# A list scheduler that counts a TensorE instruction as ready a margin behind its inputs, and a sample's loads traced one stretch later

## The chip, the cores and the metric

The kernel runs on one NeuronCore of a Trainium2 chip. The metric is device time in microseconds of one launch. A profiled execution gives a trace; its times count from the first instruction of the span. The engines are called PE (TensorE, matrix products; PEld is its weight load, which is an instruction of its own), DVE (VectorE), ACT (ScalarE), POOL (GpSimd) and SP (SyncE, which here issues every DMA). Each engine works through its own list of instructions in the order of that list.

## The reference, cut to what matters

One layer of a streaming encoder is run for a prompt of 1024 frames and for a sample of 64 new frames with caches, with the same weights:

```python
h = rms_norm(xp, g_norm1)
qa, ka, va, qb, kb, vb, logf = in_proj(h, w_in, ...)       # 8 heads A, 8 heads B, forget logits
oa = chunk_band_attn_prompt(qa, ka, va, rel_bias)          # band of 64-frame chunks, 8 chunks back
ob = forget_attn_prompt(qb, kb, vb, logf)                  # causal, cumulative forget bias
xp = xp + concat(oa, ob) @ w_o
mk, mv = mem_kv(mem_prompt, g_mem, w_mkv, g_mk)            # memory keys and values, 256 tokens
xp = xp + mem_attend(rms_norm(xp, g_norm2), mk, mv, w_mq, g_mq, w_mo)
f, conv = conv_ffn(rms_norm(xp, g_norm3), zeros, w_up, w_conv, b_conv, w_down)
xp = xp + f
# the same for the sample xs (64 frames), whose attention reads cache_a_k/v (512 rows),
# cache_b_k/v (1024 rows) and cache_mem_k/v, and whose conv reads state_conv
```

Outputs are both streams, the new keys, values and forget logits, the memory keys and values and the conv states. All is float32. The kernel makes most products as three products of split operands (`SPLIT`: high x high, low x high, high x low), which is why an operand appears as a pair such as `whi` and `wlo`.

## The kernel before

**Stages.** The program is traced, that is, written down instruction by instruction, in this order. (1) A ramp: the first projections (`pj`) and their splits. (2) For each pair of heads in turn, projections of eight 128-frame tiles, and beside them the attention of the pairs before: scores into the one tile `S` (`Attn.score`, L706), the minimum over them (`mx`, L709), the exponential (L711), transposes (`PT`, L743), their split into `pth` and `ptl` (L744, L745), and the products with `v` into `O` (L762). The queries `q` come from transposes into `tq` (L484) and two evictions (L493, L495). (3) The memory products: eight column blocks `n` of `w_mkv`, two row tiles each, in pieces of six matmuls (`mem_piece`, L829); weights come by `load_wm` (tile `mwraw`, L813) and are split on ACT and DVE (L821, L822). Beside them stand the eight samples, that is, the sample's eight pairs of heads. (4) The output product (`w_o`), memory attention and the first half of `w_mo`. (5) From `arranged` on, products of a Strassen-like scheme for the feed-forward part, in the order in which they are written.

**The samples.** `Sample.load` issues on SP the loads of one pair: `sqd` and `svn` (its own queries, keys and values, by way of DRAM), two halves of the cached keys `kraw`, and one (A) or two (B) tiles `vraw` of cached values. `load_bias` loads its bias `s` (from `rows` for A, from `negs` for B). `prep` transposes `sqd` (L1022), scales it (L1027, L1028) and, for B, works the bias over on POOL (L1031, L1034). `score` makes the products with `kraw` (L1045, L1046), the minima on DVE (L1048, L1050) and the exponential on ACT (L1056). `turn` transposes (L1069) and copies (L1073 and L1071), `sum` multiplies with `vraw` and `svn` (L1083), `out` transposes back (L1093). The order of the pairs is `SAMPLES`, B pairs first: samples 0 to 3 are B, 4 to 7 are A. Samples 0 to 3 have three `kraw` buffers, 4 to 7 four of their own.

A loop over `x` makes one stretch for each sample: it traces the score of sample `x`, the turns and sums of the sample before and the prep of sample `x + 1`, woven (`weave`) with `PER[x]` pieces of the memory products from `line`. At its head stand the bias load of sample `x + 1` and, before the change, the loads of sample `x + 3`. Samples 0, 1 and 2 are loaded earlier. In stretches 5 and 6 `load_early` loads the first tiles of the output product (`oraw`, `omix`).

**The planner.** What is traced is not what runs. At the end `arrange(tc, arranged)` takes everything traced before `arranged` (stages 1 to 4) and gives each of the five engines a new order, by simulating a list schedule. Each instruction is a node with an assumed busy time and an assumed time to its result (`cost`). Node numbers follow the traced order and are the priority: of the instructions that are ready on an engine, the one traced first goes first. A node is ready when all that it depends on is done in the simulation (results on other engines plus `signal`, 0.07 us) and when its tile has a free buffer; for a matmul behind a matmul it depends on, when that one is streamed. An SP instruction has one more condition: the matmul traced `AHEAD` (10) products ahead of it must have begun. The loop takes the engine that can start earliest. Instructions whose time has not come are in `coming[engine]`; those that are ready are in the two heaps of `waiting[engine]`, called `a` and `b` (`b` for those that need a port shared by DVE and POOL). The result is written as an order of each engine and nothing more: on the chip the engines wait by semaphores for what they need, in that order, whether or not the planned times come true.

Of the kernel before, what the change touches and what calls it, by code (L numbers as in the profile page):

```python
# [41 lines left out]
def hybrid_step(ctx: ExitStack, tc: tile.TileContext, i: dict, o: dict):  # L42
# [345 lines left out]
    def weave(main, subs):  # L388
        j = 0
        for x, f in enumerate(main):  # L390
            f()
            while j * len(main) < len(subs) * (x + 1):
                subs[j]()
                j += 1
        for f in subs[j:]:
            f()
# [539 lines left out]
    kvs, stores, waiting = {}, [], []  # L936
# [193 lines left out]
    samples = [Sample(p) for p in SAMPLES]  # L1130
# [80 lines left out]
    def open_left():  # L1211
        nonlocal stream
        left.close()
        stream = Stream(late_left.enter_context(tc.tile_pool(name="wr", bufs=1, side="left")))
        x = late_left.enter_context(tc.tile_pool(name="x0", bufs=1, side="left")).tile([P, 384], F32, name="x0")
        ha = mixes.enter_context(tc.tile_pool(name="ha", bufs=1, side="left"))
        stage = rest.enter_context(tc.tile_pool(name="stage", bufs=1, side="left"))
        mixr.extend(parts(ha, "a"))
        raws = dict(enumerate(early_mix))

        def place_of(n):
            c0, cn = CHUNKS[n // KT]
            return n % KT, slice(c0, min(c0 + cn, T))

        def load_mix(n):
            if n < KT:
                return
            k, c = place_of(n)
            raws[n] = stage.tile([P, 384], F32, name="mraw", bufs=STAGE)[:, :c.stop - c.start]
            nc.sync.dma_start(raws[n], mixd[k][:, c])  # L1230

        def split_mix(n):
            k, c = place_of(n)
            hi, lo = (mixr[z][k][:, c] for z in range(2))
            act.copy(hi, raws[n])
            dve.tensor_tensor(lo, raws[n], f32(hi), op=ALU.subtract)  # L1236
            if KT <= n and n + STAGE < 3 * KT:
                load_mix(n + STAGE)

        with tc.issue_after(samples[-1].loaded.ins):  # L1240
            for n in range(KT, KT + STAGE // 2):
                load_mix(n)
            stream.fetch()
            for n in range(KT + STAGE // 2, KT + STAGE):
                load_mix(n)
        nc.sync.dma_start(x, i["xT"][0, :, 0:384])
        assert not waiting
        for f in stores:
            f()
        return ha, [[lambda n=c * KT + k: split_mix(n) for k in range(KT)] for c in range(3)], x  # L1250
# [3 lines left out]
    def load_early(n):  # L1254
        if n < 2:
            raw = mq.tile([P, 4, P], F32, name="oraw", bufs=3)
            nc.sync.dma_start(raw, srcs[n])
            early_raws.append(raw)
        for k in range(4 * n, 4 * n + 4):
            raw = mq.tile([P, 384], F32, name="omix", bufs=KT)  # L1260
            nc.sync.dma_start(raw, mixd[k][:, 0:384])
            early_mix.append(raw)

    old, ha = [], None
    for x in range(len(samples) + 1):
        if not line and ha is None:
            ha, split, early_x = open_left()
            left_at = x
        cur = samples[x] if x < len(samples) else None
        nxt = samples[x + 1] if x + 1 < len(samples) else None  # L1270
        if nxt:
            nxt.load_bias()
        if x + 3 < len(samples):
            samples[x + 3].load()
        if x in (5, 6):
            load_early(x - 5)
        new, fin = [], []
        if cur:
            new = [cur.score]
        if nxt:  # L1280
            fin = [nxt.prep]
        subs = new[:1] + old[:2] + new[1:] + old[2:-1] + fin[:1] + old[-1:] + fin[1:]
        main = line[:PER[x]]
        del line[:PER[x]]
        if ha and x == left_at:
            pieces = first[0].pieces
            subs = new[:1] + old[:2] + split[0][:1] + new[1:] + split[0][1:2]
            subs += [lambda: stream.upto(1)] + old[2:-1] + split[0][2:4] + [lambda: stream.upto(2)]
            subs += [pieces[0], split[0][4], pieces[1], split[0][5]] + old[-1:] + [pieces[2], split[0][6], pieces[3], split[0][7]]
        elif ha:  # L1290
            main = pieces[4:] + [f for two in zip(split[1], first[1].pieces) for f in two]
            subs = [lambda: stream.upto(4)] + subs
        weave(main, subs)
        if cur:
            c = cur.nc
            old = [lambda z=z, u=cur: u.turn(z) for z in range(2)] + [lambda u=cur: u.sum(0)]
            old += ([lambda u=cur: u.turn(2), lambda u=cur: u.sum(1)] if c == 2 else [])
            old += [lambda u=cur, c=c: u.sum(c), cur.out]
# [243 lines left out]
    for n, u in enumerate(mems):  # L1542
        h, c = u.h, u.c
        a, b = (mems[n - 1] if n else None), (mems[n - 2] if n > 1 else None)
# [39 lines left out]
    def long_row(tag):  # L1584
        return row(tag, 768)[:, :H]
# [27 lines left out]
    for w, m in enumerate(ROWS):  # L1613
        x = long_row("qhi")
# [152 lines left out]
    for n, m in enumerate(ROWS):  # L1767
        x = long_row("qhi")
# [270 lines left out]
    for s, (what, f) in enumerate(steps):  # L2039
# [16 lines left out]
        for m in range(4):  # L2056
            two = [(x, z) for x in ((s,) if f < NG - 2 else (s, s + 1)) for z in range(2)]
            for x, z in sorted(two, key=lambda v: v[1]) if m == 3 and what == "M4" else two:
                la, ra = down_ops[x]
                first, final = steps[x][1] == 0, steps[x][1] == NG - 1  # L2060
                if True:
                    for y, (p, b) in enumerate(SPLIT):
                        pe.matmul(ws[m][:, z, :Q], la[p][:, m * P:(m + 1) * P], ra[b][:, z * Q:z * Q + Q],  # L2063
                                  start=first and y == 0 and what in opening, stop=final and y == 2 and what in closing, skip_group_check=True)
# [13 lines left out]
    assert not any(later.values())  # L2078
    late_left.close()
    arrange(tc, arranged)  # L2080


# [4 lines left out]
def arrange(tc, end):  # L2087

    import heapq

    signal = 0.07
    nodes, owner, made, touched, opened, closed = [], {}, {}, {}, {}, []
    writer, readers, group = {}, {}, {}
    setter = select = None
# [49 lines left out]
    for ins in traced[:end]:  # L2144
        engine, kind = str(ins.engine).split(".")[-1], type(ins).__name__
# [77 lines left out]
    after, missing, ready = [[] for _ in nodes], [len(x[2]) + len(x[3]) for x in nodes], [0.0] * len(nodes)  # L2223
    coming, free, order = ({e: make() for e in ENGINES} for make in (list, float, list))
    waiting = {e: ([], []) for e in ENGINES}
# [9 lines left out]
    def release(n):  # L2235
        for t in held[n][1] - taken:
            tag = owner[t][2]
            if not slots[tag]:
                stuck.setdefault(tag, []).append(n)
                return  # L2240
            ready[n] = max(ready[n], min(slots[tag]))
        heapq.heappush(coming[nodes[n][1]], (ready[n], n))
# [9 lines left out]
    def earliest(e):  # L2252
        a, b = waiting[e]
        return min([1e9] + [free[e]] * bool(a) + [max(free[e], port)] * bool(b) + [max(free[e], x[0]) for x in coming[e][:1]])

    while True:
        start, engine = min((earliest(e), e) for e in ENGINES)
        if start == 1e9:
            break
        while coming[engine] and coming[engine][0][0] <= start:  # L2260
            n = heapq.heappop(coming[engine])[1]
            heapq.heappush(waiting[engine][nodes[n][6]], n)
        a, b = waiting[engine]
        line = min([x for x in (a, b if port <= start else []) if x], default=None)
        if line is None:
            continue
        n = heapq.heappop(line)
        order[engine].append(n)
        _, _, _, _, busy, done, shared = nodes[n]
        free[engine] = start + busy  # L2270
        if engine == "SP":
            lane = max(lane, start + 1.4) + done
            done = lane - start + 0.3 + min(0.5, done / 2)
        if shared:
            port = start + busy
        for t in held[n][1]:
            if t not in taken:
                taken.add(t)
                slots[owner[t][2]].remove(min(slots[owner[t][2]]))
            left[t] -= 1  # L2280
            over[t] = max(over[t], start + done + signal)
            if not left[t]:
                slots[owner[t][2]].append(over[t])
                for m in stuck.pop(owner[t][2], ()):
                    release(m)
        for m, begun in after[n]:
            same = nodes[m][1] == engine
            ready[m] = max(ready[m], start + (0 if begun else busy if same and engine == "PE" else done if same and engine != "SP" else done + signal))
            missing[m] -= 1
            if not missing[m]:  # L2290
                release(m)
# [91 lines left out]
```

## Time and profile before

| | |
|---|---|
| time, median of 3 runs | 1693.71 us (1690.34 to 1694.01) |
| time of the profiled execution | 1686.39 us |
| its span, first to last instruction | 1684.6 us |
| mean granted clock of TensorE | 0.999 |
| busy PE / PEld / DVE / ACT / POOL | 1660.5 / 1613.2 / 1166.4 / 907.9 / 583.2 us |
| moved by DMA | 199.82 MB, mean 119 GB/s |

How to read it: the profiled execution is one run; its time holds its span and some 2 us around it. The median of the other runs lies 7.3 us above it. Differences inside the profile are taken within the profile. Rows of the table of windows give, for a stretch of the span, its length and the busy time of PE, PEld, DVE, ACT and POOL with their counts of instructions, then the granted clock, the mean busy share of the DMA engines and GB/s. A row of waits reads: engine, tile and line of the instruction that waited, what it waited for, us in total, times, longest. A row of a timeline gives start, length, engine, line, operation, and in brackets the idle time before it and what ended that.

### The profile page before, as it was taken

To read this page: it belongs to the slowest core of one execution; us is meant where nothing else is said; L and a number is where in the kernel's file an instruction comes from. 1 tells how busy PE (TensorE), PEld (TensorE's weight loads), DVE (VectorE), ACT (ScalarE), POOL (GpSimd) and SP (SyncE) were. 2 spreads that over 40 slices of the span, in tenths; PEclk is the share of its full clock that TensorE was granted. 3 is DMA by queue.
4 is the path that set the end of the run, shared out by engine and by line. 5 is a ranking of instruction groups with operands and counts; after the bars stand their busy time and mean duration, and the time that the engine had idled before them with its cause. 6 is when DMAs were issued, how large, how long until landed. Compare 5 with 4: busy or idle time off the path is not lost.

```text
span 1684.6 us, 33070 instructions
## 1 busy us (share of the span) xinstructions
PE 1660.5 (99%) x12027; PEld 1613.2 (96%) x12027; DVE 1166.4 (69%) x2584; ACT 907.9 (54%) x2003; POOL 583.2 (35%) x846
## 2 busy tenths in 40 slices
PE   9999999999999999999999999999999999999999
PEld 8899899999998879999999999999999999999999
DVE  7866866766778644344553797777777777559996
ACT  8866677767777564345555554333333333444442
POOL 1756688888853213444446111000000000000000
PEclk9999999999999999999999999999999999999999
DMA  7323243232235974421115632222222222983332
GB/s 242 91 77 84 76 113 91 77 92 84 64 118 165 290 216 152 141 82 58 55 58 162 214 115 84 77 78 77 78 77 77 78 78 84 320 298 120 102 109 88
DMA packets 142260, 199.82 MB, mean 119 GB/s; under 512 B 22200, under 2 KB 85304, under 8 KB 142096
## 3 DMA queue, kind: packets, MB, share of 16 engines
q1 hardware_dynamic: 142096, 197.70, 37.8%
q8 instruction: 95, 1.56, 0.4%
q14 instruction: 69, 0.57, 0.1%
HBM read 148.01 MB, written 43.34 MB: 114 GB/s over the span
## 4 chain that ended last, share of the span: by engine, by line
PE 87%; ACT 4%; DVE 4%; DMA 2%; issue 1%; SPq 0%; POOL 0%; DVEq 0%; ACTq 0%; POOLq 0%
PE W L1739 27%; PE W L2063 14%; PE pj L1183 14%; PE pj L413 11%; PE S L706 4%; PE O L762 3%; PE PT L743 3%; PE pj L829 2%; PE W L1183 1%; PE pj L535 1%; PE S L1475 1%; PE tq L1514 1%; PE O L1514 1%; PE tq L484 1%; DMA k<-k 1%
## 5 line engine op out<-in xcount | busy, mean ns | idle before, releaser
L413 PE MATMUL pj<-whi,xhi 128*128 128x384 f32 (+1 forms) x480 | 172.7, 360 | 0.0
L413 PE MATMUL pj<-whi,xlo 128*128 128x384 f32 (+1 forms) x480 | 164.7, 343 | 0.0
L413 PE MATMUL pj<-wlo,xhi 128*128 128x384 f32 (+1 forms) x480 | 164.1, 342 | 0.0
L1739 PE MATMUL W<-h,hi 128*128 128x272 f32 x704 | 134.3, 288 | 1.4 <-ACT qlo L1875 1.4
L1845 POOL COPY s<-gp 128x2 f32<-128x2 f32 x22 | 15.8, 719 | 336.1 <-DVE gp L1844 336.1
L2063 PE MATMUL W<-f,hi 128*128 128x272 f32 x672 | 127.2, 287 | 0.0
L745 DVE TENSOR_TENSOR ptl<-PT,pth 128x512 fp32r<-128x512 f32 (+2 forms) x192 | 97.9, 521 | 32.4 <-ACT pth L744 30.6
L713 POOL TENSOR_SCALAR s<-s,ssum 128x640 f32<-128x640 f32 (+7 forms) x128 | 92.9, 728 | 68.2 <-DVE ssum L712 52.2
L711 ACT ACTIVATE s<-s,mx 128x640 f32<-128x640 f32 (+7 forms) x128 | 94.5, 738 | 35.9 <-DVE mx L709 35.0
L744 ACT CAST pth<-PT 128x512 fp32r<-128x512 f32 (+2 forms) x192 | 84.6, 451 | 54.1 <-PE PT L743 52.4
L1739 PEld LDWEIGHTS W<-h,hi 128*128 128x128 f32 x704 | 110.3, 188 | 1.7 <-ACT qlo L1875 1.6
L2063 PEld LDWEIGHTS W<-f,hi 128*128 128x128 f32 x672 | 105.2, 188 | 0.1
L1739 PE MATMUL W<-h,lo 128*128 128x272 f32 x352 | 101.3, 288 | 0.0
L706 PE MATMUL S<-k,q 128*128 128x256 f32 (+3 forms) x432 | 90.5, 323 | 7.2 <-DVE mx L709 2.8
L2063 PE MATMUL W<-f,lo 128*128 128x272 f32 x336 | 96.7, 288 | 0.0
L1602 ACT CAST hi<-raw 128x512 fp32r<-128x512 f32 x68 | 42.2, 621 | 98.7 <-PE W L1739 59.2
L413 PEld LDWEIGHTS pj<-whi,xhi 128*128 128x128 f32 x480 | 90.6, 189 | 1.5
L413 PEld LDWEIGHTS pj<-wlo,xhi 128*128 128x128 f32 x480 | 90.8, 189 | 0.7
L413 PEld LDWEIGHTS pj<-whi,xlo 128*128 128x128 f32 x480 | 90.3, 188 | 0.4
L743 PE MATMUL PT<-ident,s 128*128 128x128 f32 x528 | 87.6, 273 | 0.8 <-DVE ptl L745 0.8
L706 PEld LDWEIGHTS S<-k,q 128*128 128x128 f32 x432 | 67.3, 188 | 21.8 <-DVE q L495 8.1
L1183 PE MATMUL pj<-a,hi 128*128 128x384 f32 (+1 forms) x352 | 87.2, 332 | 1.0 <-DVE a L1236 0.9
(611 smaller groups left out, 5684.3 us busy)
## 6 DMA issues: line engine op xcount, KB each, us to landing
raw<-in_w_down_dram SPq DMA_DIRECT2D x45, 256.0 KB, 2.7
wraw<-in_w_dram SPq DMA_DIRECT2D x56, 192.0 KB, 2.7
raw<-in_w_up_dram SPq DMA_DIRECT2D x41, 256.0 KB, 2.7
h<-ad SPq DMA_DIRECT2D x32, 272.0 KB, 5.1
mwraw<-in_w_mkv_dram SPq DMA_DIRECT2D x16, 512.0 KB, 5.6
raw<-in_w_mo_dram SPq DMA_DIRECT2D x32, 256.0 KB, 3.2
kvraw<-in_w_down_dram SPq DMA_DIRECT2D x32, 256.0 KB, 3.4
k<-k SPq DMA_DIRECT2D x60, 128.0 KB, 2.4
```

Source lines behind the costliest of these rows:

```text
L413: pe.matmul(pj[:, :nw], x_part(a, k, t * P, P), wt[k][b][:, :nw], start=n == 0, stop=n == 3 * KT - 1)
L706: pe.matmul(sp[:, a:a + m], q, ring[:, h, z, k0:k0 + m], start=z == 0, stop=z == 1)
L711: act.activation(s[:, :n], s[:, :n], ACT.Exp, bias=mx, scale=-1.0, accum_out=sm)
L713: pool.tensor_scalar(s[:, :n], s[:, :n], sm, 1.0, op0=ALU.mult, op1=ALU.mult)
L743: pe.transpose(pt[:, b - ch[0]], self.s[j][:, (b - w0) * P:(b - w0 + 1) * P], ident)
L744: act.copy(hi[:, f:f + n, j], pt[:, f:f + n])
L745: dve.tensor_tensor(lo[:, f:f + n, j], pt[:, f:f + n], f32(hi[:, f:f + n, j]), op=ALU.subtract)
L762: pe.matmul(op[:r, cols], v[:, :r], self.pts[b][m][:, x, cols], start=first and (b, m) == steps[0], stop=ch[-1] == self.last and (b, m) == ...
L1183: pe.matmul(out()[:, :cn], w[a][:, k % 4], x[b][k][:, c0:c0 + cn], start=k == 0 and (a, b) == SPLIT[0], stop=k == KT - 1 and (a, b) == SPL ...
L1602: act.copy(hi, t)
L1739: pe.matmul(w[:, z, :Q], a(p, j), rights[j][b][:, z * Q:z * Q + Q], start=fresh and begin and j == 0 and x == 0, stop=final and end and j ...
L2063: pe.matmul(ws[m][:, z, :Q], la[p][:, m * P:(m + 1) * P], ra[b][:, z * Q:z * Q + Q], start=first and y == 0 and what in opening, stop=fina ...
```

## The change

Two things change.

1. In the planner, `sure` gives PE a margin of 0.2 us. While PE has a ready instruction in `a` or `b`, an instruction in `coming` moves to the ready ones only if its time lies at least 0.2 us before the present start. If PE has nothing ready, the old rule holds. A matmul that depends on a matmul of PE itself gets its time 0.2 us earlier, so that the margin does not apply to it. The other engines have no margin.
2. In the loop over the samples, `samples[x + 3].load()` is traced behind the `weave` of stretch `x` instead of ahead of it.

```diff
-        if x + 3 < len(samples):
-            samples[x + 3].load()
         if x in (5, 6):
             load_early(x - 5)
...
         weave(main, subs)
+        if x + 3 < len(samples):
+            samples[x + 3].load()
...
-    signal = 0.07
+    signal, sure = 0.07, {"PE": 0.2}
...
-        while coming[engine] and coming[engine][0][0] <= start:
+        a, b = waiting[engine]
+        while coming[engine] and coming[engine][0][0] <= start - (sure.get(engine, 0.0) if a or b else 0.0):
             n = heapq.heappop(coming[engine])[1]
             heapq.heappush(waiting[engine][nodes[n][6]], n)
-        a, b = waiting[engine]
...
-            ready[m] = max(ready[m], start + (0 if begun else busy if same and engine == "PE" else done if same and engine != "SP" else done + signal))
+            ready[m] = max(ready[m], start + (0 if begun else busy - sure[engine] if same and engine == "PE" else done if same and engine != "SP" else done + signal))
```

## The prediction, as put on record before the change was run

> **What bounds the kernel now.** I read the page first: the busy times and the chain that ended last.
>
> ```profile
> span 1684.6 us, 33070 instructions
> PE 1660.5 (99%) x12027; PEld 1613.2 (96%) x12027; DVE 1166.4 (69%) x2584; ACT 907.9 (54%) x2003; POOL 583.2 (35%) x846
> PE 87%; ACT 4%; DVE 4%; DMA 2%; issue 1%; SPq 0%; POOL 0%; DVEq 0%; ACTq 0%; POOLq 0%
> ```
>
> TensorE is the bound. No multiplication is added or taken away, so only time in which PE stands still can be won or lost: 1684.6 - 1660.5 = 24.1 us of visible idle time, and whatever hides inside a "busy" PE, since a matmul's modelled end covers short gaps. Next, the table of windows, cut where the stages of the program change:
>
> ```profile
> 0.00:20.00 20.00, 17.93 (x96) 17.60 (x97) 13.72 (x35) 15.91 (x35) 0.70 (x6) 1.00 0.92 308
> 20.00:60.00 40.00, 35.69 (x219) 32.32 (x217) 35.57 (x121) 37.13 (x106) 21.88 (x31) 1.00 0.51 151
> 60.00:520.00 460.00, 455.53 (x3013) 430.60 (x3014) 331.69 (x920) 325.76 (x837) 347.65 (x544) 1.00 0.31 86
> 520.00:640.00 120.00, 112.34 (x800) 100.11 (x799) 74.54 (x211) 76.37 (x213) 20.83 (x30) 0.99 0.80 236
> 640.00:950.00 310.00, 309.62 (x2093) 304.10 (x2092) 139.02 (x367) 152.99 (x360) 140.53 (x143) 1.00 0.36 111
> 950.00:1684.60 734.60, 729.34 (x5816) 728.47 (x5814) 571.84 (x934) 299.78 (x458) 51.57 (x94) 1.00 0.35 116
> ```
>
> The columns are length, busy time of PE, PEld, DVE, ACT and POOL, the granted clock, the DMA share and GB/s. Visible PE idle is 2.1 us at the start, 4.3 in the ramp, 4.5 in the long stage of projections with attention beside them, 7.7 in the stage of memory products and samples (DMA share 0.80), 0.4 after it, 5.3 in the rest. The planner whose rule is changed orders only what is traced before about 950 us, so 18 to 19 us of visible idle lie in its reach. PEld, the weight loads, shows more: 29.4 us idle in 60:520. The waits of PEld there, and in 640:950:
>
> ```profile
> PEld S L706 <- DVE q L495: 8.1, 23, 0.8
> PEld S L706 <- DVE mx L709: 4.4, 8, 0.7
> PEld PT L1498 <- POOL s L1490: 3.7, 20, 0.4
> ```
>
> So 31 scores (L706) were issued before their input was there, for 8.1 + 4.4 = 12.5 us, 0.40 us each: either q had just been written or the one score tile had just been read out. One such place on the timeline, below the row of one of the three kinds of projection matmuls in that stage:
>
> ```profile
> L413 PE MATMUL pj<-whi,xhi 128*128 128x384 f32 x448 | 161.2, 360 | 0.0
> 364.62 0.34 PE L413 MATMUL pj<-whi,xlo 128*128 128x384 f32 x1
> 364.62 0.19 PEld L413 LDWEIGHTS pj<-whi,xhi 128*128 128x128 f32 x1
> 364.79 0.34 PE L413 MATMUL pj<-whi,xhi 128*128 128x384 f32 x1
> 365.48 0.30 PEld L706 LDWEIGHTS S<-k,q 128*128 128x128 f32 x2 [0.67 <-DVE mx L709]
> 365.48 0.51 PE L706 MATMUL S<-k,q 128*128 128x512 f32 x1 [0.35 <-DVE mx L709]
> ```
>
> Projection matmuls start 0.17 us apart (364.62, 364.79); the score starts 0.69 later. PE lost 0.69 - 0.17 = 0.52 us where PEld shows 0.67 idle: a wait of PEld costs PE its length less 0.15. Other projections were ready, but the engine takes its list in order.
>
> **The change, part by part.**
>
> Part 1, the margin. While PE has something ready, the planner now offers it only what was ready 0.2 us before (the diff's figure, about one weight load of the rows, 0.19). A just-ready score then stands one or two matmuls later. Nothing is added on the chip: no instruction, no wait, no DMA; PE's successors of its own matmuls are exempted (busy - 0.2). What a later score costs is covered by projections, 1344 of which (448 of each kind) stand in this stage; without that cover (ramp, end of attention) the rule does not apply, for it needs another ready instruction.
>
> (a) 60:520: the 31 waits cost PE 31 x (0.40 - 0.15) = 7.8 us. A margin of 0.2 takes at most 0.2 from each and nothing from those under 0.15; I take 0.15 on average, 31 x 0.15 = 4.6 us. Ends: 0, if the delay moves with the plan, and 7.8.
>
> (b) 640:950: 20 transposes (L1498) waited for POOL for 3.7 us, 0.185 each; by the same rule 20 x 0.035 = 0.7 us. Ends 0 and 3.7, the whole wait.
>
> (c) 20:60: ACT and DVE are over 88% busy and PE rarely has a choice. I take 0.5 of the 4.3 us; ends a loss of 1 (a new order of a latency chain) and a gain of 2.
>
> (d) 520:640: the waits of PE are few and long.
>
> ```profile
> PE S L706 <- DMA k<-k: 2.1, 1, 2.1
> PE PT L977 <- DVE kv L958: 1.7, 1, 1.7
> PE O L1083 <- ACT pth L1073: 1.5, 1, 1.5
> ```
>
> 0.2 off each of these is 0.6; I take 0.5; ends 0 and 1.
>
> Part 2, the loads. Sample x+3's loads move from ahead of stretch x to behind it, for x = 0 to 4. Each is sqd, svn, two kraw and one or two vraw: five or six SP instructions. They are moved past that stretch's memory products, their stores and, in stretches 0, 2 and 3, two mwraw loads; they now stand directly ahead of the next bias, the last of them also ahead of the early omix loads. But an SP instruction may be planned once the tenth product ahead of it has begun, and behind stretch x is the same gate as ahead of stretch x+1. So each boundary now has sample x+2's loads and then the bias, where it had the bias and then sample x+3's. The place where this bites is near 588:
>
> ```profile
> 555.33 1.11 SPq L1001 DMA_DIRECT2D kraw<-in_cbk_dram  x2
> 581.22 0.59 SPq L996 DMA_DIRECT2D sqd<-sqk  x1
> 584.85 0.38 SPq L813 DMA_DIRECT2D mwraw<-in_w_mkv_dram  x1
> ```
>
> ```profile
> 589.38 0.62 ACT L821 CAST mwhi<-mwraw 128x512 fp32r<-128x512 f32 x1 [3.29 <-DMA mwraw<-in_w_mkv_dram]
> 590.28 0.24 ACT L1073 COPY pth<-PT 64x128 f32<-64x128 f32 x1
> 590.57 0.48 PE L1083 MATMUL O<-svn,pth 64*128 64x128 f32 x2 [1.52 <-ACT pth L1073]
> 525.00:530.00 5.00, 2.88 (x24) 2.68 (x23) 2.98 (x8) 1.99 (x7) 0.07 (x1) 1.00 0.48 107
> 555.00:560.00 5.00, 4.56 (x32) 3.99 (x33) 4.29 (x16) 4.39 (x11) 0.27 (x1) 1.00 1.05 312
> 590.00:595.00 5.00, 4.43 (x23) 4.08 (x24) 2.96 (x5) 4.09 (x13) 0.00 (x0) 0.73 0.52 162
> 595.00:600.00 5.00, 5.00 (x38) 4.33 (x37) 1.76 (x7) 1.41 (x4) 0.00 (x0) 0.93 0.63 163
> ```
>
> SP issues one sample's loads for 584.85 - 581.22 = 3.6 us and then the last weights; ACT stands 3.29 us for them with pth queued behind, and PE 1.52 for pth. Right after it the clock falls: 5 x (1 - 0.73) + 5 x (1 - 0.93) = 1.7 us lost.
>
> (e) By the argument of the gates, mwraw still has a sample's loads ahead of it, now those of sample 5 (counted from 0) where it had those of sample 6. What really changes is that the first load moved, 512 KB of kraw at 555.33, leaves a full queue (share 1.05 at 312 GB/s), and one sample's bytes are added where the share is 0.63. So the stall may shorten; I take an even chance that the half clock goes, 0.8 us. Ends: a gain of 1.5 + 1.7 = 3.2, and the loss of the second rival.
>
> [...]
>
> The loads' lateness costs nothing by itself; what covers it is their lead:
>
> ```profile
> 594.04 1.25 SPq L1001 DMA_DIRECT2D kraw<-in_cak_dram  x2
> 619.27 1.13 PE L1045 MATMUL S<-kraw,sq 128*128 128x512 f32 x2 [0.77 <-ACT sq L1027]
> kraw<-in_cbk_dram SPq DMA_DIRECT2D x8, 256.0 KB, 4.2
> s<-negs SPq DMA_DIRECT2D x8, 272.0 KB, 6.2
> 603.78 1.85 SPq L1261 DMA_DIRECT2D omix<-mixd  x4
> 618.36 0.52 ACT L1235 CAST a<-omix 128x384 fp32r<-128x384 f32 x1
> ```
>
> The last sample's kraw has 25 us; a stretch (about 9 us here) later it still has 16, against landings that took 4 to 6. The early omix loads, now behind them on SP, have 14.6 us and lose 3.6. Were the lead gone, the score, ACT's su and the samples' chain would wait for a landing.
>
> Sum: 4.6 + 0.7 + 0.5 + 0.5 + 0.8 = 7.1 us. Against the profiled execution (span 1684.6, time 1686.39) that is 1679.3. The median shown, 1693.71, is 7.3 us above that execution; the saving is PE time and should hold there too: 1693.7 - 7.1 = 1686.6.
>
> **The rivals.**
>
> First, nothing measurable: the waits are the plan's errors, and errors follow a new plan. If q and mx come late by what PE is moved, (a) and (b) give 0 to 2 us and the rest cancels: 1692 to 1694. For it: the waits reach 0.8 us, four margins. Against it: the margin is added only on PE's side, and the planner's times for DVE do not change.
>
> Second, slower: a bias now stands behind a sample's loads on SP.
>
> ```profile
> 560.07 1.92 SPq L1016 DMA_DIRECT2D s<-negs  x2
> 570.19 0.52 POOL L1034 TENSOR_SCALAR_AFFINE_SELECT s<-s 64x64 f32<-64x64 f32 x2
> 571.23 1.23 DVE L1048 CUSTOM_DVE_ANT_0 s<-S,s 128x1024 f32<-128x1024 f32 x1 [0.20 <-PE S L1045]
> ```
>
> Sample 2's bias is ready on POOL at 570.71 and read by DVE at 571.23: a slack of 0.5 us. With 3.6 us of SP ahead of it and 512 KB more before it in a full queue (1.7 us at 300 GB/s), it would come up to 5.3 us later; DVE, queued behind it the mwlo splits, ACT's exponential and PE's transposes of that sample would stand 4.8 us, which surely costs a half clock or two (1.7 each): up to 8 us. Less 4.6 for (a) that is +3.6: 1697. It decides once the bias lands 2 us later than now. Against it: that sample's kraw was issued at 555.33, ahead of the bias at 560.07, before too, so in a full queue the same bytes lie ahead of it in either order.
>
> Third, the loads do all they might: the stall at 588 goes with its clock, 3.2 in place of 0.8: 1684.
>
> **How the numbers follow.** 0.2% of this time, 3.4 us, is what a measurement can tell from no change. Forecast with the third rival (a saving of 3.4 to 14): 0.58. Nothing measurable: 0.27. Slower: 0.15, nearly all of it the second rival. The forecast's own range is 1680 to 1690. For 8 in 10 I leave some 0.07 below 1680 (all upper ends at once: 7.8 + 3.7 + 2 + 1 + 3.2 = 17.7, 1676) and 0.13 above 1696.5.
>
> **What would show it.** In the profile after: PEld's waits before L706 in 60:520 fall from 12.5 us to about 6, with fewer than 31 of them; those before L1498 from 3.7 to below 1; PE's busy count is the same and 60:520 holds some 25 more matmuls; the last kraw is issued near 602 in place of 594; 590:600 shows a clock of 1.00, or the fall stays. The prediction is wrong if the L706 waits keep their sum, if DVE's L1048 waits for POOL by microseconds, or if new clock falls appear in 540:640.

## The result, and the profile after

On one chip, in turn: before 1693.45 us (median of six runs, 1688.96 to 1695.15), after 1680.93 us (six, 1679.49 to 1687.95). The ratio is 0.9937 [0.9916, 0.9958]. The medians differ by 12.5 us, the means by 10.6, which fits the ratio. In a second measurement (after_again below) the medians differ by 10: 1679.75 against 1689.73, ratio 0.9942 [0.9926, 0.9957]. Three executions of the experiments below (one each of margin_attn, rest_loads and the kernel before) were slow, at 2286 to 5490 us, and no figure here counts them.

The profiled execution of after is the slowest of its six runs (1687.95 us). That of before was the fastest seen of that kernel until then. Laid side by side, the two profiles show a loss of 1.6 us. Lines from the page of after:

```profile
span 1686.2 us, 33049 instructions
...
PE 1659.8 (98%) x12027; PEld 1616.6 (96%) x12027; DVE 1160.3 (69%) x2584; ACT 908.2 (54%) x2003; POOL 584.1 (35%) x846
...
PE 80%; DVE 6%; DMA 6%; ACT 5%; issue 2%; SPq 1%; POOL 0%; DVEq 0%; ACTq 0%
```

PE's instruction count is the same and its busy time within 0.7 us. The chain of waits leaves PE more often (80% in place of 87%). The windows of this execution, cut as for before, show where:

```profile
20.00:60.00 40.00, 37.00 (x226) 33.44 (x225) 35.36 (x121) 37.35 (x109) 21.55 (x32) 1.00 0.52 154
60.00:520.00 460.00, 454.73 (x3043) 434.33 (x3041) 334.10 (x926) 329.98 (x843) 351.43 (x548) 1.00 0.32 88
520.00:640.00 120.00, 110.83 (x756) 97.22 (x757) 69.53 (x202) 72.30 (x202) 16.42 (x24) 0.96 0.76 224
640.00:950.00 310.00, 308.87 (x2095) 304.60 (x2094) 134.11 (x365) 151.77 (x359) 140.90 (x143) 1.00 0.35 112
```

60:520 holds 30 more matmuls than before (3043 against 3013), and 20:60 seven more. Then 520:640 holds 44 fewer (756 against 800) at a clock of 0.96, which alone is 120 x 0.04 = 4.8 us. The trace's record of the clock has it at half rate three times there, from 525.1, 559.3 and 593.4 us, each time for 3413 ns, that is 1.7 us lost each time. The profile of before had one such fall. Another execution of the same changed kernel (the one profiled in the experiments, span 1677.7) has none:

```profile
60.00:520.00 460.00, 455.78 (x3054) 436.11 (x3054) 336.04 (x929) 331.65 (x847) 351.15 (x548) 1.00 0.33 89
520.00:640.00 120.00, 114.02 (x805) 101.69 (x805) 71.60 (x205) 75.02 (x207) 20.63 (x27) 1.00 0.80 241
590.00:595.00 5.00, 5.00 (x43) 4.80 (x43) 0.01 (x1) 1.99 (x7) 0.00 (x0) 1.00 0.37 121
595.00:600.00 5.00, 5.00 (x37) 4.28 (x37) 1.73 (x8) 2.39 (x7) 0.00 (x0) 1.00 0.78 207
```

So one order of instructions gives spans 8.5 us apart: three falls (5.1 us), and 3.2 us more of PE standing visibly in 520:640 (120 - 110.83 against 120 - 114.02). A saving of 10 us can't be read from one profile of each kernel. What can be read is how often an engine waited in the stages before the falls. PEld's waits of after in 60:520 and in 640:950:

```profile
PEld S L706 <- DVE q L495: 3.6, 11, 0.5
PEld S L706 <- DVE mx L709: 2.4, 4, 1.0
PEld PT L743 <- DVE ptl L745: 2.4, 5, 0.9
...
PEld W L1650 <- POOL sq L1599: 1.2, 1, 1.2
...
PEld PT L1498 <- POOL s L1490: 0.4, 2, 0.3
```

The 31 late scores of 12.5 us are now 15 of 6.0, the 20 late transposes of 3.7 us now 2 of 0.4. New are transposes that wait for `ptl` (0.5 us before) and one wait in memory attention, L1650 for `sq`.

### The profile page after: what moved, and what is told of

It is laid out like the page before. It is cut to its first block, busy times and chain, and to the rows that moved or that the text cites. A ratio compares the mean times of both kernels' runs of the same rounds, so it can differ in the third digit from the quotient of the medians.

```text
span 1686.2 us, 33049 instructions
## 1 busy us (share of the span) xinstructions
PE 1659.8 (98%) x12027; PEld 1616.6 (96%) x12027; DVE 1160.3 (69%) x2584; ACT 908.2 (54%) x2003; POOL 584.1 (35%) x846
## 4 chain that ended last, share of the span: by engine, by line
PE 80%; DVE 6%; DMA 6%; ACT 5%; issue 2%; SPq 1%; POOL 0%; DVEq 0%; ACTq 0%
PE W L1739 27%; PE pj L1183 13%; PE W L2063 12%; PE pj L413 10%; PE S L706 3%; PE O L762 3%; PE PT L743 3%; PE pj L829 2%; PE pj L535 1%; DMA mwraw<-in_w_mkv_dram 1%; DMA wraw<-in_w_dram 1%; PE S L1475 1%; PE tq L1514 1%; DMA k<-k 1%; PE O L1514 1%
## 5 line engine op out<-in xcount | busy, mean ns | idle before, releaser
L743 PE MATMUL PT<-ident,s 128*128 128x128 f32 x528 | 95.6, 274 | 2.5 <-DVE ptl L745 1.5
L706 PE MATMUL S<-k,q 128*128 128x256 f32 (+3 forms) x432 | 92.3, 322 | 4.4 <-DMA k<-k 2.1
L1602 ACT CAST hi<-raw 128x512 fp32r<-128x512 f32 x68 | 42.2, 621 | 98.8 <-PE W L1739 59.4
L1183 PE MATMUL pj<-a,hi 128*128 128x384 f32 (+1 forms) x352 | 83.8, 330 | 1.5 <-DVE a L1236 1.2
L706 PEld LDWEIGHTS S<-k,q 128*128 128x128 f32 x432 | 70.5, 190 | 13.3 <-DVE q L495 3.6
```

What stands on the lines that cost most here:

```text
L706: pe.matmul(sp[:, a:a + m], q, ring[:, h, z, k0:k0 + m], start=z == 0, stop=z == 1)
L743: pe.transpose(pt[:, b - ch[0]], self.s[j][:, (b - w0) * P:(b - w0 + 1) * P], ident)
L1183: pe.matmul(out()[:, :cn], w[a][:, k % 4], x[b][k][:, c0:c0 + cn], start=k == 0 and (a, b) == SPLIT[0], stop=k == KT - 1 and (a, b) == SPL ...
L1602: act.copy(hi, t)
```

## The experiments

Three theories stood against each other. The margin theory (A): waits of the weight loads for inputs that had just become ready are what the change removes. The loads theory (B): the later loads, and the clock falls that go with their stalls, bring it. The theory of chance (C): any new order of the list would have moved the time as much.

The table holds what was measured. Each ratio is to the kernel before on the same chip, with its 95% interval. Then come the median time; the time from the first to the last matmul of L535, which frames the projections with attention beside them; the sum of PEld's waits before L706 for `q` and `mx` there; the half clock in the profiled execution, counted in lengths of 3413 ns (a fall of 6827 ns is two); the start of its first L1650, less 1.7 us for each such length up to there, which is the planned part without the clock's share; and the mean clock over all runs, of which each is known to 0.001, about one length.

| kernel | ratio | median us | L535, us | L706 waits, us | half clock, lengths | L1650 less half clock, us | clock |
|---|---|---|---|---|---|---|---|
| before (profile of the prediction) | | | 458.2 | 12.5 | 1 | 935.0 | |
| after (profile above) | 0.9937 [0.9916, 0.9958] | 1680.93 | 455.7 | 6.0 | 3 | 931.5 | 0.9990 |
| before_again | 0.9998 [0.9984, 1.0011] | 1689.77 | 458.6 | 12.6 | 3 | 934.9 | 0.9978 |
| after_again | 0.9942 [0.9926, 0.9957] | 1679.75 | 454.0 | 5.8 | 0 | 926.8 | 0.9990 |
| margin_only | 0.9962 [0.9947, 0.9977] | 1682.85 | 454.0 | 5.7 | 1 | 928.9 | 0.9980 |
| loads_only | 0.9984 [0.9973, 0.9995] | 1686.24 | 458.1 | 12.5 | 0 | 933.7 | 0.9990 |
| margin_attn | 0.9951 [0.9936, 0.9965] | 1681.03 | 454.3 | 6.0 | 2 | 930.3 | 0.9990 |
| margin_04 | 0.9962 [0.9948, 0.9975] | 1683.5 | 449.2 | 4.1 | 4 | 926.9 | 0.9965 |
| first_load | 0.9988 [0.9978, 0.9998] | 1688.2 | 457.6 | 12.2 | 2 | 934.6 | 0.9981 |
| rest_loads | 0.9979 [0.9970, 0.9989] | 1686.23 | 457.8 | 12.4 | 0 | 936.4 | 0.9990 |
| attn_04 | 0.9920 [0.9903, 0.9937] | 1675.09 | 449.5 | 4.1 | 2 | 925.0 | 0.9995 |
| attn_07 | 0.9931 [0.9913, 0.9948] | 1677.15 | 448.1 | 2.0 | 2 | 927.2 | 0.9983 |
| signal_09 | 1.0008 [0.9993, 1.0023] | 1691.32 | 458.5 | 8.5 | 1 | 935.3 | 0.9972 |
| load_behind_bias | 0.9975 [0.9962, 0.9988] | 1686.12 | 458.1 | 12.5 | 0 | 933.7 | 0.9987 |

The four rows from before_again to loads_only were measured beside 29 runs of before (median 1689.73, 1684.19 to 1694.47), the next four beside 24 (1689.98), both on one chip; the last four were measured on another chip beside 22 (1690.08).

### The two parts, each alone

margin_only is the changed kernel with the loads put back:

```diff
             nxt.load_bias()
+        if x + 3 < len(samples):
+            samples[x + 3].load()
...
         weave(main, subs)
-        if x + 3 < len(samples):
-            samples[x + 3].load()
```

> The margin of 0.2 us alone; the loads stay at the head of their stretch. Theory A (the gain is PE's waits for inputs that the plan had just ready): ratio 0.993 to 0.995, nearly the whole change, and PEld's waits before L706 in 60:520 fall to about half of 12.5 us as in the changed kernel. Theory B (the gain is the later loads): ratio 0.998 to 1.002. Theory C (any new order of this plan moves the time by as much, up or down): anything from 0.993 to 1.007, not tied to the waits of L706.

Measured: 0.9962, 6.9 us between the medians. That is clear of no change, and a smaller gain than the 0.993 to 0.995 that theory A expected. Its PEld waits in 60:520:

```profile
PEld S L706 <- DVE q L495: 3.5, 11, 0.5
PEld S L706 <- DVE mx L709: 2.2, 4, 1.0
```

These are those of after: the whole effect on the late scores belongs to the margin, and the stage is shorter by 458.2 - 454.0 = 4.2 us.

loads_only is the kernel before with only the loads moved, the reverse of the diff above:

> The later place of the loads alone, no margin. Theory A: ratio 0.998 to 1.001 (my term for it was 0.8 us, 0.05%); the L706 waits stay at about 12.5 us and the L1498 waits at about 3.7. Theory B: 0.993 to 0.995. Theory C: anything from 0.993 to 1.007. The rival that a bias comes late: above 1.002, with DVE L1048 waiting for POOL by microseconds.

Measured: 3.5 us saved, where the prediction had 0.8: by its ratio (0.9984) inside theory A's range, and far from theory B's. The order of PE's instructions is that of before, row by row; SP's differs, and DVE's and ACT's in three or four places each. The waits before L706 are untouched (8.1 and 4.4). PE's waits in 520:640, and the windows in which before lost its clock:

```profile
PE PT L977 <- DVE kv L958: 1.7, 1, 1.7
PE S L706 <- DMA k<-k: 1.6, 1, 1.6
PE S L1045 <- ACT sq L1027: 1.3, 2, 0.7
```

```profile
590.00:595.00 5.00, 5.00 (x38) 4.26 (x37) 2.81 (x9) 3.75 (x11) 0.00 (x0) 1.00 0.64 173
595.00:600.00 5.00, 5.00 (x43) 4.80 (x43) 0.76 (x2) 1.52 (x6) 0.00 (x0) 1.00 0.48 154
```

The wait for `pth` is gone, and so is the fall behind it. The 40 runs of before on that chip (the 29 and the 11 of before_again) have a mean time of 1689.5 us and a mean clock of 0.9979, loads_only 1686.5 and 0.9990. Of the 3.0 us between the times the clocks account for (0.9990 - 0.9979) x 1685 = 1.9 us. Over the 29 runs of before, time and lost clock go together (correlation 0.80, 0.9 us of time for each us of lost clock).

### The repeats

before_again and after_again are the two kernels unchanged.

> The kernel before once more, unchanged, for its clock falls and a second profile. Its shown runs lie 3 to 9 us above the profiled execution (1686.39 us, one fall of the clock of 3.4 us). If falls of the clock make that spread: most runs here have a mean clock of 0.997 to 0.998 (three or more falls, 1.7 us each) and a time near 1690 to 1695, and a run with 0.999 has one near 1687. If the clock has no part in it: the clock is 0.999 in all and the time spreads all the same. Ratio 0.998 to 1.002 in either case.

> The changed kernel once more, unchanged. Ratio 0.992 to 0.996. Its profiled execution of 1687.95 us had a clock of 0.997 and the other five 0.999 to 1.000 at 1679.5 to 1682.2. If falls of the clock explain that one: a profile here with a clock of 0.999 or 1.000 has a span near 1679 and no half clock in 520:600, and any run with 0.997 lies some 5 us above those with 1.000.

before_again gives 0.9998: what two kernels differ by when nothing differs. Its profile has three falls, with PE standing 2.2 us for `pth`:

```profile
PE O L1083 <- ACT pth L1073: 2.2, 1, 2.2
PE S L706 <- DMA k<-k: 2.0, 1, 2.0
PE PT L977 <- DVE kv L958: 1.7, 1, 1.7
```

So the good profile of before was luck, as the bad one of after was. after_again gives 0.9942, and the parts alone multiply to 0.9962 x 0.9984 = 0.9946: within the intervals they add, and neither needs the other.

### A new order without the margin

signal_09 is the kernel before with another assumed time for a semaphore:

```diff
-    signal = 0.07
+    signal = 0.09
```

> The kernel before (no margin, loads where they were) with the planner's time for a signal between engines 0.09 in place of 0.07 us: a plan about as different from that of before as the margin's, that does not let PE's inputs be more than 0.02 us early. Theory C (any new order moves the time as much): ratio anywhere from 0.993 to 1.007, its L535 stage away from 458 us by 3 or more. Theory A: 0.998 to 1.002, 457 to 459 us there, L706 waits 11 to 13 us.

Measured: 1.0008, no change, although at some 1400 of the 12027 places in PE's order another product stands than in before. (In margin_only it is some 2900 places, so this order is about half as different.) Its PEld waits in 60:520, and the window:

```profile
PEld S L706 <- DVE mx L709: 4.7, 9, 0.9
PEld S L706 <- DVE q L495: 3.8, 11, 0.8
PEld PT L743 <- DVE ptl L745: 2.3, 6, 0.6
PEld tq L484 <- POOL qk L359: 1.8, 2, 1.5
PEld S L706 <- issue: 1.6, 4, 0.6
```

```profile
60.00:520.00 460.00, 453.94 (x3007) 429.98 (x3008) 331.08 (x919) 325.51 (x834) 346.99 (x541) 1.00 0.31 86
```

The waits for `q` halve here too, so that 8.5 us are left before L706 where theory A expected 11 to 13. But those for `ptl`, for `qk` and for nothing shown grow, all idle time of PEld in the window is 460 - 429.98 = 30.0 us (29.4 in before), and the stage stays at 458.5 us. The planner's times shift and its errors shift with them, as the first rival of the prediction said of the margin. So a new order alone need not bring 7 us. One such order can't show that none does; the sizes of the margin tried below speak against it.

### Where the margin works

margin_attn is the changed kernel with the margin only for what is traced before the memory products:

```diff
     weights.close()
+    staged = len(nc.cur_bb.bb.instructions)
...
+    mark = 0
+    for at, ins in enumerate(traced[:end]):
+        if at <= staged:
+            mark = len(nodes)
...
-        while coming[engine] and coming[engine][0][0] <= start - (sure.get(engine, 0.0) if a or b else 0.0):
+        while coming[engine] and coming[engine][0][0] <= start - (sure.get(engine, 0.0) if (a or b) and coming[engine][0][1] < mark else 0.0):
```

> The changed kernel, but the margin holds only for instructions traced ahead of the memory products (ramp and the stage of projections with attention); behind that the old rule. If the margin's gain lies in that stage, as the traces say (its last projection matmul starts at 511.6 in place of 518.1 us, and what follows the samples takes 1.2 us longer with the margin): ratio 0.993 to 0.995 against the kernel before, 0 to 1.5 us better than the changed kernel, and the stretch from the last L1093 to the first L1650 is back from 304.0 to 302.8 us. If the margin helps everywhere (my terms b and d): 1 to 2 us worse than the changed kernel, ratio 0.995 to 0.996.

Measured: 0.9951, within the interval of the whole change, and so at the border between the two expectations. What the margin does behind the attention is worth nothing that these runs can tell. In the profiles the stretch behind the samples, from the last L1093 (the samples' end) to the first L1650, takes 302.7 us in before, 304.1 in after, 304.0 in after_again and 302.6 here, although the late transposes are back (PEld L1499, the former L1498, waits for POOL 3.7 us in 21 places). That is no price of the margin as such: the stretch takes 302.8 us in margin_04, which has a margin there, and 303.9 in signal_09, which has none. It goes with the order that a plan happens to get there.

margin_04 is the changed kernel with twice the margin everywhere:

```diff
-    signal, sure = 0.07, {"PE": 0.2}
+    signal, sure = 0.07, {"PE": 0.4}
```

> The changed kernel with a margin of 0.4 us in place of 0.2. If the margin works by the size of the lateness (31 scores, 0.40 us late on average): the waits of PEld for q and mx before L706 fall from 5.8 to 1 to 3 us and the last projection matmul starts another 1 to 3 us sooner, near 509.5; ratio 0.991 to 0.994. If 0.2 was all because it covers one weight load (0.19 us): no further gain, 0.994 to 0.996, waits as with 0.2. If any new order would do: not tied to the waits.

Measured: 0.9962, no better than half the margin, and yet the stage of L535 takes 449.2 us, 9.0 less than before. Of the late scores 4.1 us are left, where 1 to 3 were expected. The gain was paid back in 520:640, whose clock is 0.94 (three falls, one of them 6827 ns long). PE's waits there:

```profile
PE S L1045 <- ACT sq L1027: 4.3, 2, 3.7
PE PT L977 <- DVE kv L958: 3.3, 1, 3.3
```

Both waits are the longest of their kind in the profiles shown. The likely reason is that in the samples a margin puts the chain from PE to ACT and DVE and back later, and no projections stand there to cover it; no run separates that from the new order.

attn_04 and attn_07 put the two together: margin_attn with 0.4 and with 0.7 in place of 0.2.

> Later loads, and a margin of 0.4 us for the ramp and the stage of projections with attention alone (the kernel with 0.4 everywhere won another 5 us there, 449.2 us from the first to the last L535 in place of 454, and lost them among the samples). If the stages add up: 449 us in that stage, ratio 0.991 to 0.9935, better than the changed kernel by 2 to 5 us. If a plan's gain in one stage is paid back in the next (later scores, later k copies): 449 us there and a ratio of 0.994 to 0.997.

> The same with 0.7 us. The waits before L706 were up to 0.8 us long, 0.40 on average, and 4.1 us of them are left with 0.4. If lateness is what the margin takes: another 1 to 2 us at most in that stage (447 to 449 us), ratio 0.990 to 0.9935. If the margin costs by holding scores back: 449 to 453 us and a ratio above that with 0.4.

Measured: 0.9920 [0.9903, 0.9937] and 0.9931 [0.9913, 0.9948]. PEld's waits of attn_04 in 60:520, and the window:

```profile
PEld S L706 <- DVE mx L709: 2.4, 5, 0.8
PEld S L706 <- DVE q L495: 1.7, 6, 0.4
PEld PT L743 <- DVE ptl L745: 1.5, 5, 0.4
```

```profile
60.00:520.00 460.00, 457.93 (x3074) 440.72 (x3073) 342.72 (x939) 332.55 (x854) 352.58 (x549) 1.00 0.32 89
```

3074 matmuls in the window, 61 more than before. By the dose 0, 0.2, 0.4, 0.7 the late scores cost 12.5, 6.0, 4.1 and 2.0 us and the stage takes 458, 454, 449.5 and 448.1. With 0.7 scores begin to wait for the keys' DMA instead (L706 for `k`: 2.1 us in 4 places) and PE for `pth` again (1.8 us). The medians of 0.4 and 0.7 differ by 2.1 us, which is the difference of their mean clocks (0.0012 x 1680 = 2.0), and the intervals overlap, so which of the two is better is open. attn_04 has the lowest median of all, 1675.09 us, 15.0 below before, where after is 10 to 12.5 below its own runs of before. Its interval and those of after overlap, so that it beats before is shown, and that it beats after is likely.

The sum of all idle time of PEld in the window follows the stage better than the two rows before L706 do. It is 29.4 us in before, 25.7 in after, 23.9 in after_again, 19.3 in attn_04, and 18.6 with 0.7:

```profile
60.00:520.00 460.00, 457.48 (x3081) 441.42 (x3081) 339.81 (x936) 332.75 (x854) 349.95 (x547) 1.00 0.32 89
```

### Which load, and lateness or order

first_load moves only sample 3's load, rest_loads only those of samples 4 to 7, both in the kernel before. The edit of first_load (that of rest_loads is its complement):

```diff
-        if x + 3 < len(samples):
+        if x and x + 3 < len(samples):
             samples[x + 3].load()
...
         weave(main, subs)
+        if not x:
+            samples[3].load()
```

> The kernel before (no margin), with only sample 3's loads moved behind stretch 0; those of samples 4 to 7 stay at the heads of their stretches. Theory L1, my step (e): what counts is that this load's kraw leaves the full queue at 555 us. Then nearly all of the later loads' gain stands: ratio 0.998 to 0.999, mean clock 0.999, PE's wait for pth near 588 under 1 us. Theory L2: the later loads count, each out of the way of its own stretch's weights: ratio 0.999 to 1.001, the wait near 588 about 2 us and the clock falls as before (mean 0.998).

> The kernel before (no margin), with the loads of samples 4 to 7 moved behind their stretches and sample 3's left at the head of stretch 0: the complement of the kernel with the first load alone. L1: ratio 0.9995 to 1.001, PE's wait for pth near 588 about 2 us, mean clock 0.998. L2: 0.998 to 0.999, that wait under 1 us, mean clock 0.999.

Measured: 1.8 us (0.9988) and 3.7 us (0.9979). The prediction had named the first load, whose 512 KB leave a full queue (DMA share 1.05 at 312 GB/s in 555:560 of before), as the one that matters. By these medians it brings about half of what the later ones bring; the intervals overlap. Neither theory's signs came whole: first_load has the time of L1 and the wait and clock of L2, rest_loads the time and clock of L2 and the wait of L1. The wait for `pth` lasts 1.8 us in first_load, with a fall behind it, and in rest_loads it is as long as ever, with none (a window and a row of the timeline of rest_loads):

```profile
590.00:595.00 5.00, 3.15 (x22) 2.74 (x23) 2.74 (x5) 4.00 (x11) 0.00 (x0) 1.00 0.42 148
```

```profile
591.85 0.37 PE L1083 MATMUL O<-svn,pth 64*128 64x128 f32 x1 [2.09 <-ACT pth L1073]
```

This execution lost no clock and its planned part is no shorter than that of before (936.4 against 935.0), so its gain over the median of before is, in this execution, the falls that it does not have.

load_behind_bias loads each of the samples 3 to 7 one stretch later, as the change does, but behind the next bias instead of ahead of it:

```diff
-        if x + 3 < len(samples):
-            samples[x + 3].load()
+        if x and x + 2 < len(samples):
+            samples[x + 2].load()
```

> The kernel before (no margin), with each moved load one stretch later, as in the change, but behind the next bias on SP in place of ahead of it. If the gain of the later loads is their lateness: ratio 0.9975 to 0.999, mean clock 0.999, as with the loads moved alone. If it is that the loads go ahead of the bias: 0.9995 to 1.001, mean clock 0.998.

Measured: 0.9975, within loads_only's interval. This is the cleanest of the comparisons: the orders of PE, DVE, ACT and POOL are those of before, row by row, and only SP's differs, in some 80 of 1677 places. Its profile again shows no wait for `pth` and no fall. So it is the lateness of the loads that helps, whichever side of the bias they stand on.

## Why the prediction was right, and where it was not

The sign and the forecast's own range (1680 to 1690) held, the range only just: 1680.93 against 1686.6. The mechanism of part 1 is shown for the stage of projections with attention. The size came out larger mainly because of step (e).

**(a), 4.6 us for the late scores.** The stage is 2.5 to 4.2 us shorter in the four profiles with a margin of 0.2 (455.7, 454.0, 454.0, 454.3 against 458.2; PE's order up to its end is the same in all four), and the waits fell to what was foretold (about 6 us, fewer than 31 places). What the step had too low is how far a larger margin reaches. With 0.4 the stage gives 9 us, more than the 7.8 that the step had as the price of all late scores. Its rule that a wait costs its length less 0.15 us was read at one place. In the sums, PEld's idle time in 60:520 falls by 10.1 us from before to attn_04, 8.4 of them in the two rows, and the stage by 8.7; from before to after_again by 5.5 and 4.2. So the rule takes off too much, and with 0.4 the two rows are most of the fall but not all of it.

**(b), 0.7 us for the transposes of L1498: wrong sign.** The waits went as foretold (3.7 to 0.4 us), and the stretch around them became 1.3 us longer, where the step had no loss among its ends. margin_attn, without the margin there, gets it back; margin_04, with twice the margin, does too (302.8 us, and 2.6 us of those waits). Of the places where PE stood instead, the profile of after shows the one before L1650, 1.2 us. A group of many short waits, each hardly longer than what PE's matmuls cover (0.185 us against 0.15), was no loss to begin with: by the prediction's own rule each cost 0.035 us.

**(c), 0.5 us for the ramp.** Its end is 2.0 to 2.6 us earlier in margin_only, after and after_again (57.4 to 57.6 against 59.5 to 60.0), but 59.0 in margin_attn and 59.4 and 59.6 with 0.4. PE's order there is the same in margin_attn as in the first three, so the execution matters as much as the rule.

**(d), 0.5 us for 520:640.** It can't be told apart: falls of the clock and differences of some 3 us between executions of one order cover it. In margin_04 PE stood longer there (4.3 and 3.3 us) than any gain set down for this step.

The sum of (a) to (d), 6.3 us, stands against 6.9 us measured for the margin alone. That it came so near is partly luck. From the profile of before to that of margin_only, half clock taken off, the way to the first L1650 is 6.1 us shorter: 2.6 in the ramp, 4.1 in the stage, 0.8 among the samples, and 1.4 longer behind them. The figures of (c), (a), (d) and (b) were 0.5, 4.6, 0.5 and 0.7 gained, and errors of some 2 us in (b) and (c) cancel.

**(e), 0.8 us for the loads: mis-sized.** Measured alone 3.5 us, which is about the 3.2 us of the third rival, by a way of which one half was foretold. Its picture, the stall at 588 gone and its half clock with it, is what loads_only and load_behind_bias show; in the changed kernel the stall is 1.4 us in one execution, with a fall behind it, and 0.5 in the other, with none. Foretold were the stall at 588 and its half clock, and that the clock's share is 1.7 us. The even chance was too timid: with the loads late the execution has fewer falls on average (clock 0.9990 for 0.9979), not one less at one place. And the reason given, one 512 KB load that leaves a full queue, is a part at most: rest_loads has the gain without it, and first_load alone brings 1.8 us. Why loads that stand later on SP save falls although a wait of 2.1 us stays is settled by no run here. What the runs leave is that the gain needs no new order on any other engine.

The second rival, a late bias, did not come about: no row of DVE's waits at L1048 in after names POOL, and loads_only has 1.0 us in one place (before 0.9). Its half clock or two for a stand of 4.8 us stays an estimate: the longest wait of PE in the rows above is 3.7 us (margin_04). The signs set out: the last `kraw` was issued at 603.77 (foretold near 602), the clock in 590:600 is 1.00 in after_again, while in the profile of after the fall stayed and new ones appeared in 520:640. That last was named as a sign that the prediction is wrong. It was a bad sign, since before_again has three falls too. The falls of after came behind gaps of 2.08 us (524.19), 1.60 (557.03) and 1.40 (591.19) in PE's work:

```profile
524.19 0.62 PE L706 MATMUL S<-k,q 128*128 128x384 f32 x2 [2.08 <-DMA k<-k]
557.03 0.41 PE L977 MATMUL PT<-ident,kv 128*128 128x128 f32 x2 [1.60 <-DVE kv L958]
591.19 0.48 PE L1083 MATMUL O<-svn,pth 64*128 64x128 f32 x2 [1.40 <-ACT pth L1073]
```

These are PE's rows of after ahead of its three falls (525.1, 559.3, 593.4).

## What to carry to other kernels

A list for an engine that works in order should not put an instruction at the very moment at which its input is due, as long as other work can stand there; size the margin by the lateness that the trace shows (here 0.40 us on average; 0.4 had the lowest median of the three margins tried, with 0.7 not told apart from it), and give it only to the stage that has such work (0.4 there alone gave 0.9920, and 0.9962 everywhere). Run the parts of a change alone before believing the one profile of the whole, and look at the clock of several executions first: here a profile with three half-clock stretches, beside a lucky one of before, turned a saving of 10 us or more into an apparent loss. Loads whose data had a lead of many microseconds (in after the last `kraw` is issued at 603.77 us and the first product with it begins at 619.83) went later on the issuing engine here at no cost that the runs show, and the time fell.

## What the runs showed of the hardware that was not expected

In the profiles here each fall of the clock inside the work lasts 3413 ns at half rate (in 525.15:528.56 of after the clock is 0.50), or twice that (6827 ns, once each in margin_attn, margin_04 and attn_04, whose clocks in 520:640 are 0.97, 0.94 and 0.97). In after the falls begin 34.13 us apart, ten such lengths, twice; in before_again, by the clock of its 5-us windows (0.88 in 525:530, 0.87 in 590:595, 0.78 in 625:630), some 64.9 us apart, nineteen such lengths, and then 34.1, ten. Where PE stands 1.4 to 2.1 us, a fall follows in some executions and not in others, behind the same wait: a 2.09-us gap without one in rest_loads (clock 1.00 in 590:600), a 1.40-us gap with one in after.

How long PE worked ahead of a fall does not tell the places with a fall from those without. In after PE was busy for 1.34, 1.47 and 2.22 of the 3.41 us ahead of its three falls, in before for 1.89 of those ahead of its one. In 56.38:59.79 and 524.00:527.41 of before it was busy for 1.81 and 1.98, at a clock of 1.00, and no fall followed. (PE's ends are modelled, so these sums are rough.) What decides is shown by no run here. The half clock in one profile goes from none to four lengths, 1.7 us lost in each, which is a large part of the 10 us by which 29 runs of the kernel before differ.

The planner's heap `b` takes DVE and POOL to share a port. What the trace of before shows of that is a POOL copy of two lengths (L1846, 128x2): 0.18 us at 1005.26, where DVE was idle from 1005.27 on, and 0.66 us at 1007.59, where a DVE instruction of 0.68 us (L1711) had begun at 1007.53. The long copy ended 0.04 us behind it.
